# Reading turned blocks back later, attending later still, and sending some blocks through GpSimd's DMA queue

## The chip, the core and the metric

The kernel runs on one core of one Trainium2 chip. TensorE (PE) multiplies, VectorE (DVE) and ScalarE (ACT) work elementwise, GpSimd (POOL) does a little of both, and SyncE (SP) issues nearly all DMAs. The five run at once, each through its own instructions in order, and wait for each other by semaphores. The metric is the device time of one execution in microseconds; 408.61 us is the median of three runs before the change (406.73 to 408.71).

## The reference

One decoder layer, all float32, 256 tokens of width 1024. The projection gives u (512 wide) and q, k, v of 8 attention heads of width 64. u goes through a causal pooling mixer. The sequence is one block of 256, so that the attention is plain causal attention within it.

```python
z = h @ w_in[l]
pool_out = multiscale_pool(u, w_pool[l], pool_scale[l])
attn_out = moba_attention(q, k, v).reshape(B_, S_, ATTN_WIDTH)
mix = jnp.concatenate([pool_out, attn_out], axis=-1) @ w_out[l]
h = layer_norm(DEEPNORM_ALPHA * h + mix, ln1_g[l], ln1_b[l])
h = layer_norm(DEEPNORM_ALPHA * h + memory_cross_attention(h, mem, w_xq[l], w_xkv[l], w_xo[l]), ...)
h = layer_norm(DEEPNORM_ALPHA * h + swiglu(h, w_gate[l], w_up[l], w_down[l]), ln3_g[l], ln3_b[l])
```

The cross-attention has 4 heads of width 256 over 256 memory tokens. The SwiGLU is 2816 wide.

## The kernel before

Precision. A float32 product is made of three faster ones: each operand is split into a high part (a cast on ACT) and a low part (a difference on DVE), and PE multiplies high by high, high by low and low by high. `split` (L318) does this for activations, `Stream.prepare` (L87) for weights.

Weights. All of them are one `Stream` of chunks of 512 KB. A chunk is loaded by SP into one of 7 raw buffers (w20r, say), cast by ACT (w20h, L99), differenced by DVE (w20l, L100). The load of chunk i + 7 (L80) is issued when chunk i is split, since it takes its raw buffer. So the order in which the splits stand on DVE sets when SP can go on, and whatever stands behind such a load on SP waits with it. Chunks w15 to w18 belong to u, w19 to w26 to xk (the memory's keys), w27 to w34 to the output projection of the mixer, w35 to w42 to xv (the memory's values), w43 to w50 to the queries of the cross heads, w51 to w58 to their output projection, w59 and up to the SwiGLU.

Order. Nothing is scheduled: engines run the instructions in the order in which the Python code emits them. Each projection is a generator that yields after a step, and `run(gen, n)` emits n steps. For u, xk and the queries a step is 3 matmuls, for xv 6. Other work is emitted between such calls, so that the sequence of `run` calls (L548 to L589, L707 to L721, L773 to L804) is a hand-written order for all engines at once.

The hop. PE wants some matrices with the other axis on the partitions. Instead of transposing them on PE, the kernel lets DVE turn 32x32 blocks, writes them to HBM with one DMA, and reads them back with four, which put the blocks at their places: `turned` (L335) and `landed` (L346). All these DMAs are on SP's queue, among the weight loads. It is done for the mixer's attention probabilities, by pairs of heads (ps is turned, pd is the copy in HBM, pt what is read back; `probs_out`, `probs_in`, `attend`), for the two 128-token halves of norm 1's output (hs, hd, hr; `h1_out`, `h1_in`, `h1_split`), and for cross heads 0 and 1 (xs, xd, xr; `xprobs_out`, `xprobs_in`, `xprobs_split`). Cross heads 2 and 3 are transposed by PE (`xprobs_pe`, L756).

Stages. q and k; then v; then u and xk with the attention's scores, hops and products (`attend`, the po tiles) and the pooling (`pool_diff`, `mix_pool`) between their steps; the mixer's output projection; norm 1 on DVE while PE goes on with xv; the queries of the four cross heads (pxq), each with its scores (xs), softmax and hop; the products with xv (xo) between steps of the cross output projection; norm 2; SwiGLU; norm 3. The memory's activations are split in two halves (`split_mem(0)`, `split_mem(4)`, tiles mTh and mTl), of which each xk chunk pair wants both. A norm (`Norm`, L597) takes its sums out of PE's banks, and its power of -1/2 (L622) is made on POOL, whose only other work behind the start is the pooling's window sums (L508, L510).

Of the kernel before, what the change touches and what calls it, by code (L numbers as in the profile page):

```python
# [18 lines left out]
KD = D // P  # L19
# [106 lines left out]
def decoder_layer(  # L126
# [3 lines left out]
    nc = tc.nc  # L130
# [78 lines left out]
    def split_mem(k):  # L209
        split(mT[0][:, k:k + 4, :], mT[1][:, k:k + 4, :], mr[0][:, k:k + 4, :])  # L210
# [99 lines left out]
    def run(gen, n=None):  # L310

        while n is None or n > 0:
            if next(gen, gen) is gen:
                return False
            n = None if n is None else n - 1
        return True

    def split(h, l, ps):  # L318
        nc.scalar.copy(h, ps)  # L319
        nc.vector.tensor_sub(l, ps, r32(h))  # L320
# [11 lines left out]
        split(dst[0][:, k0:k0 + 4, ts], dst[1][:, k0:k0 + 4, ts], ps.rearrange("p (k t) -> p k t", k=4))  # L332


    def turned(blocks, n, name):  # L335

        st = sp.tile([P, 4, n, 32], F32, name=f"{name}s", tag="pair", bufs=3)
        for at, src in blocks:
            m = src.shape[1]
            nc.vector.transpose(st[:, :, at:at + m, :].rearrange("p j m b -> p m j b"),  # L340
                                src.rearrange("p m (j b) -> p m j b", b=32))
        via = hp.tile([P, 4, n * 32], F32, name=f"{name}d")
        nc.sync.dma_start(via, st.rearrange("p j m b -> p j (m b)"))
        return via

    def landed(via, n, name, raw=None):  # L346

        if raw is None:
            raw = sp.tile([P, 4, n, 32], F32, name=f"{name}r", tag="pair", bufs=3)
        for j in range(4):  # L350
            nc.sync.dma_start(raw[32 * j:32 * (j + 1)].rearrange("p i m b -> p i (m b)"),
                              via[:, j, :].rearrange("(i a) r -> a i r", i=4))
        return raw

# [91 lines left out]
    def scores(hq, t):  # L446
        w = (t + 1) * P
        pss = [bank(f"ps{j}").rearrange("p (h s) -> p h s", h=2) for j in range(2)]
        for h in range(2):
            for j in range(2):  # L450
                hs = slice(j * HD, (j + 1) * HD)
                hp = 2 * hq + h
                nc.tensor.matmul(pss[j][:, h, :w], qT[hs, hp, t * P:(t + 1) * P], kT[hs, hp, :w],
                                 start=True, stop=True)
        todo = []
        for j in range(2):
            pr = sp.tile([P, 2, S], F32, name="pr", bufs=PR_BUFS)[:, :, :w]
            mx = sp.tile([P, 2], F32, name="mx", bufs=6)
            for h in range(2):
                nc.vector.tensor_tensor_reduce(pr[:, h, :], pss[j][:, h, :w], tri[:, S - w:], -1.0, -NEG,  # L460
                                               op0=OP.add, op1=OP.min, accum_out=mx[:, h:h + 1])
            todo.append((pr, exps(pr, pr, mx, -1.0)))
            probs[hq, t, j] = pr
        for pr, sm in todo:
            scaled(pr, sm)
# [6 lines left out]
    def probs_out(hp):  # L472
        blocks = []
        for j in range(2):
            for t in range(T):
                pr = probs[hp // 2, t, j][:, hp % 2]
                blocks.append((3 * j + t, pr.rearrange("p (m c) -> p m c", c=P)))
        turns[hp] = turned(blocks, 6, "p")

    def probs_in(hp):  # L480
        if hp % 2 == 0:
            homes[hp // 2] = ap.tile([P, 2, KD * P], F32, tag="a8", name=f"pt{hp // 2}")
        raw = homes[hp // 2][:, hp % 2, :4 * 6 * 32].rearrange("p (i m b) -> p i m b", i=4, m=6)
        raw = landed(turns[hp], 6, "p", raw).rearrange("p i m b -> p m i b")
        pts[hp] = [(raw[:, 3 * j:3 * j + 2], raw[:, 3 * j + 2]) for j in range(2)]
# [3 lines left out]
    def attend(hp):  # L489
        po = bank("po")  # L490
        for j in range(2):
            hs = slice(j * HD, (j + 1) * HD)
            vs = slice((2 * hp + j) * HD, (2 * hp + j + 1) * HD)
            s0, s1 = pts[hp][j]
            out = po[hs, :S].rearrange("p (t i b) -> p t i b", t=T, i=4)
            nc.tensor.matmul(out, vt[:, 0, vs], s0, start=True, stop=False)  # L496
            nc.tensor.matmul(out[:, 1], vt[:, 1, vs], s1, start=False, stop=True)  # L497
        split(cT[0][:, 4 + hp, :], cT[1][:, 4 + hp, :], po[:, :S])
# [14 lines left out]
    def pool_diff(g):  # L513
        pl = upad[:, g, PADW:]
        nc.vector.scalar_tensor_tensor(pl, sums[g][:, PADW:], 1.0 / WINDOWS[g], pl, op0=OP.mult, op1=OP.subtract)

    def mix_pool(g):
        pm = bank("pm")
        nc.tensor.matmul(pm[:, :S], wpl[:, g, :], upad[:, g, PADW:], start=True, stop=True)
        nc.scalar.activation(cT[0][:, g, :], pm[:, :S], AF.Copy, bias=0.0, scale=psc[:, g:g + 1])  # L520
        nc.vector.scalar_tensor_tensor(cT[1][:, g, :], pm[:, :S], psc[:, g:g + 1],
                                       r32(cT[0][:, g, :]), op0=OP.mult, op1=OP.subtract)
# [25 lines left out]
    v, u, xk = do_v(), do_u(), do_xk()  # L548
# [3 lines left out]
    run(v, 4)  # L552
    scores(0, 1)
    run(v)
    probs_out(0)
    run(u, 6)
    scores(1, 0)
    probs_in(0)
    probs_out(1)
    run(u, 10)  # L560
    scores(1, 1)
    probs_in(1)
    split_mem(0)
    run(u, 8)
    attend(0)
    pool_diff(0)
    pool_diff(1)
    run(u, 4)
    probs_out(2)
    split_mem(4)  # L570
    run(u)
    attend(1)
    run(xk, 12)
    probs_in(2)
    probs_out(3)
    mix_pool(0)
    run(xk, 8)
    mix_pool(1)
    pool_diff(2)
    probs_in(3)  # L580
    run(xk, 8)
    attend(2)
    mix_pool(2)
    pool_diff(3)
    ws.pace = 2
    run(xk, 10)
    attend(3)
    mix_pool(3)
    run(xk)  # L589
    ws.pace = 1  # L590

# [54 lines left out]
    def project(chunks, get, held, pieces=PIECES):  # L646

        acc = {piece: accbank("acc") for piece in PIECES}  # L650
        if pieces != PIECES:
            (*_, (_, _, c), _), last = pieces, PIECES[-1]
            acc[pieces[-2]], acc[pieces[-1]] = acc[last][:, :c - last[1]], bank("acc")[:, :last[2] - c]
        head, rest = chunks[:-held], chunks[-held:]
        done = sum(ws.rows(numbers) for numbers in head)
        if head:
            yield from proj_rows(acc, head, get, PIECES, True, pieces != PIECES, True)
        ws.prepare(ws.used + AHEAD)
        ws.prepare(ws.used + W_BUFS, nc.gpsimd)
        ws.held = True  # L660
        for piece in pieces:
            yield from proj_rows(acc, rest, lambda k: get(done + k), [piece], not head or piece[1] % 512 != 0, True,
                                 piece == pieces[-1], bool(head) and pieces != PIECES)
            yield piece, acc[last] if pieces != PIECES and piece == pieces[-2] else acc[piece]
# [8 lines left out]
    load_norm("g", 1, ln1_g)()  # L673
    load_norm("b", 1, ln1_b)()
    h1 = ap.tile([P, T, D], F32, tag="a8", name="h1")
    mix = project(c_mix, lambda k: (cT[0][:, k], cT[1][:, k]), 4)
    for t in range(T):
        norm = Norm(1, xt[:, t, :], h1[:, t, :])
        for half in HALVES:
            norm.add(*half, until(mix)[1])  # L680
        norm.finish()
    run(mix)
    ws.held = False
    h1T = (a8("h1Th", F32R), a8("h1Tl", F32R))
# [7 lines left out]
        for t, c0, c1 in PIECES:  # L692
            split(xv[0][:, t, c0:c1], xv[1][:, t, c0:c1], acc[t, c0, c1])

    def h1_out(t):
        via[t] = turned([(0, h1[:, t, :].rearrange("p (k b) -> p k b", k=KD))], KD, "h")

    def h1_in(t):
        via[t] = landed(via[t], KD, "h")

    def h1_split(t):
        raw = via[t].rearrange("p i k b -> p k i b")
# [1 line left out]
            h, l = [h[:, k0:k0 + 4, t * P:(t + 1) * P].rearrange("p k (i b) -> p k i b", i=4) for h in h1T]  # L704
            split(h, l, raw[:, k0:k0 + 4])

    via = {}  # L707
    gv = do_xv()
    run(gv, 1)
    h1_out(0)  # L710
    run(gv, 3)
    h1_in(0)
    run(gv, 2)
    h1_out(1)
    run(gv, 2)
    h1_split(0)
    run(gv, 1)
    h1_in(1)
    run(gv, 3)
    h1_split(1)  # L720
    run(gv)  # L721

# [2 lines left out]
    xqT, xpr, xpt = {}, {}, {}  # L725
# [16 lines left out]
        xpr[h] = pr  # L742

    def xprobs_out(h):
        via[h] = turned([(0, xpr[h].rearrange("p s t b -> p (s t) b"))], 4, "x")

    def xprobs_in(h):
        via[h] = landed(via[h], 4, "x")

    def xprobs_split(h):  # L750
        raw = via[h].rearrange("p i m b -> p m i b")
# [21 lines left out]
    xq = [do_xq(h) for h in range(XH)]  # L773
# [4 lines left out]
    xprobs_out(0)  # L778
    run(xq[2], 5)
    xscores(1)  # L780
    run(xq[2], 3)
    xprobs_in(0)
    run(xq[2])
    xprobs_out(1)
    run(xq[3], 5)
    xprobs_split(0)
    xscores(2)
    xprobs_in(1)
    run(xq[3], 1)
    xattend(0)  # L790
    run(xq[3])

    h2 = ap.tile([P, T, D], F32, tag="a8", name="h2")
    xo = project(c_xo, lambda k: (oT[0][:, k], oT[1][:, k]), 4)
    xprobs_split(1)
    xprobs_pe(2)
    run(xo, 3)
    xscores(3)
    xattend(1)
    xattend(2)  # L800
    run(xo, 3)
    xprobs_pe(3)
    run(xo, 2)
    xattend(3)  # L804


# [149 lines left out]
```

## Time and profile before

| | |
|---|---|
| median of three runs | 408.61 us (406.73 to 408.71) |
| the profiled execution | 408.14 us, span 406.4 us |
| PE busy | 376.0 us, 93% |
| DVE, ACT, POOL busy | 254.6, 178.3, 18.0 us |
| mean granted clock of PE | 0.969 of full |
| DMA | 78.21 MB, mean 192 GB/s; 77.48 MB of it on SP's queue |

The span is from the first instruction to the last; the execution's own time is 1.7 us more. Starts and durations in a timeline are in us from the span's start. A value in brackets is how long the engine stood idle before that instruction, with what ended the wait; where the named engine had long been done, it was another, often a DMA. SPq is SP's queue of instructions: its rows give the time that the issue took, not the transfer. The grouped list of DMAs gives the median time from issue to landing. In a row of a stretch, the busy time of PE, its weight loads, DVE, ACT and POOL is followed by PE's granted clock, the share of the 16 DMA engines and the GB/s.

### The profile page before, as it was taken

How to read it: one execution, taken by the hardware profiler on the slowest of the kernel's cores; microseconds unless marked ns; L12 is line 12 of the kernel's file. 1: busy time of each engine (PE TensorE's matmuls, PEld its weight loads, DVE VectorE, ACT ScalarE, POOL GpSimd, SP SyncE). 2: the span in 40 equal slices, each digit the busy share in tenths (PEclk: the TensorE clock that was granted, in tenths of full speed). 3: DMA queues.
4: the chain of work that ended last, by engine and by line, in shares of the span. 5: the costliest groups of instructions: out<-in, count | busy, mean ns of one | idle time of the engine just before them, and what ended most of it. 6: DMA issues, size and time to landing. Idle time of an engine off the chain costs nothing.

```text
span 406.4 us, 5467 instructions
## 1 busy us (share of the span) xinstructions
PE 376.0 (93%) x2072; PEld 325.8 (80%) x2072; DVE 254.6 (63%) x376; ACT 178.3 (44%) x259; POOL 18.0 (4%) x31
## 2 busy tenths in 40 slices
PE   9999954999999719999999999999999999999992
PEld 9997953999888519999887888888888888888882
DVE  5768985665489328676488965555555464544165
ACT  4757572364342226545414654444544444334100
POOL 1000055000010000000000000000000000000000
PEclk9999996999999958999999999999999999999997
DMA  8995878767606975554210984545556655440002
GB/s 256 414 411 188 248 257 259 234 204 255 234 21 188 348 239 195 198 179 156 104 52 6 334 330 166 200 166 197 184 185 239 230 199 185 178 155 0 2 23 80
DMA packets 27225, 78.21 MB, mean 192 GB/s; under 512 B 3136, under 2 KB 8384, under 8 KB 27072
## 3 DMA queue, kind: packets, MB, share of 16 engines
q1 hardware_dynamic: 26624, 77.48, 54.9%
q10 hardware_dynamic: 576, 0.39, 0.3%
q8 instruction: 16, 0.26, 0.3%
q14 instruction: 9, 0.07, 0.1%
HBM read 73.66 MB, written 4.19 MB: 192 GB/s over the span
## 4 chain that ended last, share of the span: by engine, by line
PE 59%; DVE 5%; DMA 5%; issue 1%; ACT 0%; SPq 0%; DVEq 0%; ACTq 0%
PE pg L256 9%; PE pg L258 9%; PE pg L257 9%; PE acc L258 7%; PE acc L257 7%; PE acc L256 7%; PE pxq L274 6%; DMA w49r<-in_w_xq 2%; DMA hd<-hs 2%; PE pgt L837 1%; DMA hr<-hd 1%; DVE st L614 1%; DVE h L633 1%; PE xo L257 1%; DVE r L627 1%
## 5 line engine op out<-in xcount | busy, mean ns | idle before, releaser
L622 POOL TENSOR_TENSOR rs<-rs,mhalf 128x1 f32<-128x1 f32 x6 | 5.4, 892 | 328.2 <-DVE rs L621 328.2
L830 ACT ACTIVATE sg<-pg 128x256 f32<-128x256 f32 x22 | 8.4, 384 | 12.9 <-PE pg L258 12.8
L274 PE MATMUL pxq<-h1Th,w43h 128*128 128x256 f32 x8 | 3.4, 420 | 11.1 <-ACT h1Th L319 11.1
L496 PE MATMUL po<-pt,vt 128*64 128x256 f32 x16 | 3.1, 465 | 10.1 <-DMA pt<-pd 8.0
L611 DVE SCALAR_TENSOR_TENSOR r<-h,acc 128x256 f32<-128x256 f32 (+1 forms) x10 | 5.1, 520 | 10.9 <-PE acc L258 10.9
L831 DVE TENSOR_TENSOR sg<-sg,pg 128x256 f32<-128x256 f32 x22 | 9.3, 421 | 4.0 <-ACT sg L830 2.6
L274 PEld LDWEIGHTS pxq<-h1Th,w43h 128*128 128x128 f32 x8 | 2.6, 320 | 11.5 <-ACT h1Th L319 11.5
L320 DVE TENSOR_TENSOR h1Tl<-hr,h1Th 128x512 fp32r<-128x512 f32 x4 | 2.6, 688 | 14.0 <-ACT h1Th L319 14.0
L319 ACT CAST h1Th<-hr 128x512 fp32r<-128x512 f32 x4 | 2.3, 616 | 19.9 <-DMA hr<-hd 19.9
L429 ACT ACTIVATE pr<-pr,mx 128x128 f32<-128x128 f32 (+1 forms) x16 | 7.1, 444 | 7.3 <-DVE mx L460 7.3
L496 PEld LDWEIGHTS po<-pt,vt 128*64 128x64 f32 x16 | 1.0, 152 | 10.7 <-issue 8.2
L319 ACT CAST gTh<-pgt 128x512 fp32r<-128x512 f32 x11 | 6.0, 589 | 5.8 <-PE pgt L837 5.8
L614 DVE BATCH_NORM_STATS2 st<-r 128x6 f32<-128x512 f32 (+1 forms) x14 | 8.1, 580 | 0.5
L320 DVE TENSOR_TENSOR gTl<-pgt,gTh 128x512 fp32r<-128x512 f32 x11 | 7.1, 687 | 2.0 <-ACT gTh L319 1.5
L319 ACT CAST h2Th<-tp 128x512 fp32r<-128x512 f32 x4 | 2.3, 587 | 13.5 <-PE tp L330 13.4
L429 ACT ACTIVATE xpr<-xs,mx 128x256 f32<-128x256 f32 x8 | 3.7, 470 | 9.5 <-DVE mx L440 9.5
L627 DVE SCALAR_TENSOR_TENSOR r<-r,mv,g 128x512 f32<-128x512 f32 x11 | 7.8, 744 | 0.0
L319 ACT CAST cTh<-po 128x256 fp32r<-128x256 f32 x4 | 1.5, 372 | 12.7 <-PE po L497 12.7
L508 POOL TENSOR_TENSOR win<-upad 128x271 f32<-128x271 f32 x4 | 3.9, 968 | 53.3 <-ACT upad L536 53.3
L837 PEld LDWEIGHTS pgt<-ident,sg 128*128 128x128 f32 x44 | 5.2, 140 | 0.8
L837 PE MATMUL pgt<-ident,sg 128*128 128x128 f32 x44 | 5.8, 272 | 0.0
L633 DVE SCALAR_TENSOR_TENSOR h<-r,rs,b 128x512 f32<-128x512 f32 x8 | 5.6, 746 | 0.0
(1089 smaller groups left out, 1425.6 us busy)
## 6 DMA issues: line engine op xcount, KB each, us to landing
pd<-ps SPq DMA_DIRECT2D x4, 384.0 KB, 6.1
pt<-pd SPq DMA_DIRECT2D x16, 96.0 KB, 3.7
g<-in_ln_g SPq DMA_DIRECT2D x3, 512.0 KB, 5.1
b<-in_ln_b SPq DMA_DIRECT2D x3, 512.0 KB, 5.9
wr<-in_w_qkv SPq DMA_DIRECT2D x5, 256.0 KB, 4.2
mr<-in_mem_t SPq DMA_DIRECT2D x1, 1024.0 KB, 10.8
xt<-in_x SPq DMA_DIRECT2D x1, 1024.0 KB, 7.2
hd<-hs SPq DMA_DIRECT2D x2, 512.0 KB, 5.8
```

The lines of the kernel that those rows point to most:

```text
L256: nc.tensor.matmul(ps, wa, ya, start=start, stop=False, skip_group_check=part)
L257: nc.tensor.matmul(ps, wa, yb, start=False, stop=False, skip_group_check=part)
L258: nc.tensor.matmul(ps, wb, ya, start=False, stop=stop, skip_group_check=part)
L274: nc.tensor.matmul(pss[f], w[:, s], y, start=k == 0 and f == 0 and n == 0, stop=k == KD - 1 and n == 2, skip_group_check=True)
L319: nc.scalar.copy(h, ps)
L320: nc.vector.tensor_sub(l, ps, r32(h))
L429: nc.scalar.activation(dst[:, j, :], src[:, j, :], AF.Exp, bias=mx[:, j:j + 1], scale=sign, accum_out=sm[:, j:j + 1])
L614: nc.vector.bn_stats(self.st[:, self.n, :], self.r[:, c0:c1])
L627: nc.vector.scalar_tensor_tensor(r, r, self.mv[:, 0:1], gb["g", self.i][:, s], op0=OP.subtract, op1=OP.mult)
L633: nc.vector.scalar_tensor_tensor(self.dst[:, s], r, self.rs, gb["b", self.i][:, s], op0=OP.mult, op1=OP.add)
L831: nc.vector.tensor_mul(sg, sg, ps[:, CW:])
L837: nc.tensor.transpose(pt[:, f, t * P:(t + 1) * P], sgs[c][:, t, f * P:(f + 1) * P], ident)
```

## The change

It has three parts. First, in the mixer, `scores(1, 0)` and `probs_out(0)` change places, the reads `probs_in` come later, and the products `attend` later still: before, pairs 0 and 1 are attended among u's steps and at xk's start; now after 12 and 16 steps of xk. `split_mem(4)` comes earlier, ahead of the first pooling differences. Second, norm 1's halves are turned and written right behind each half's norm instead of among xv's steps, and these DMAs, reads too, are issued by GpSimd. Third, cross heads 0, 1 and now 2 hop, all through GpSimd's queue; head 2 is not transposed by PE any more, and the products with xv stand later: head 0's behind the last query chunk, head 1's behind four steps of the output projection, heads 2 and 3 together at its end.

```diff
-    def turned(blocks, n, name):
+    def turned(blocks, n, name, queue=nc.sync):
...
-        nc.sync.dma_start(via, st.rearrange("p j m b -> p j (m b)"))
+        queue.dma_start(via, st.rearrange("p j m b -> p j (m b)"))
...
-    def landed(via, n, name, raw=None):
+    def landed(via, n, name, raw=None, queue=nc.sync):
...
-            nc.sync.dma_start(raw[32 * j:32 * (j + 1)].rearrange("p i m b -> p i (m b)"),
+            queue.dma_start(raw[32 * j:32 * (j + 1)].rearrange("p i m b -> p i (m b)"),
...
     run(v)
+    run(u, 6)
+    scores(1, 0)
     probs_out(0)
     run(u, 6)
-    scores(1, 0)
-    probs_in(0)
     probs_out(1)
-    run(u, 10)
     scores(1, 1)
-    probs_in(1)
     split_mem(0)
     run(u, 8)
-    attend(0)
+    probs_in(0)
+    run(u, 4)
+    split_mem(4)
     pool_diff(0)
     pool_diff(1)
     run(u, 4)
+    probs_in(1)
+    run(u)
+    run(xk, 4)
     probs_out(2)
-    split_mem(4)
-    run(u)
+    run(xk, 8)
+    mix_pool(0)
+    probs_out(3)
+    attend(0)
+    run(xk, 4)
     attend(1)
-    run(xk, 12)
-    probs_in(2)
-    probs_out(3)
-    mix_pool(0)
-    run(xk, 8)
+    run(xk, 4)
     mix_pool(1)
     pool_diff(2)
+    probs_in(2)
+    run(xk, 4)
     probs_in(3)
-    run(xk, 8)
-    attend(2)
+    run(xk, 6)
     mix_pool(2)
     pool_diff(3)
     ws.pace = 2
-    run(xk, 10)
+    run(xk, 8)
+    attend(2)
+    mix_pool(3)
+    run(xk, 8)
     attend(3)
-    mix_pool(3)
...
+    via = {}
+
+    def h1_out(t):
+        via[t] = turned([(0, h1[:, t, :].rearrange("p (k b) -> p k b", k=KD))], KD, "h", nc.gpsimd)
+
+    def h1_in(t):
+        via[t] = landed(via[t], KD, "h", queue=nc.gpsimd)
+
...
         norm.finish()
+        h1_out(t)
+        if t == 1:
+            h1_in(0)
+    h1_in(1)
     run(mix)
...
-    via = {}
     gv = do_xv()
-    run(gv, 1)
-    h1_out(0)
-    run(gv, 3)
-    h1_in(0)
-    run(gv, 2)
-    h1_out(1)
-    run(gv, 2)
+    run(gv, 7)
     h1_split(0)
-    run(gv, 1)
-    h1_in(1)
-    run(gv, 3)
+    run(gv, 5)
     h1_split(1)
...
-        via[h] = turned([(0, xpr[h].rearrange("p s t b -> p (s t) b"))], 4, "x")
+        via[h] = turned([(0, xpr[h].rearrange("p s t b -> p (s t) b"))], 4, "x", nc.gpsimd)
...
-        via[h] = landed(via[h], 4, "x")
+        via[h] = landed(via[h], 4, "x", queue=nc.gpsimd)
...
     xscores(1)
-    run(xq[2], 3)
     xprobs_in(0)
     run(xq[2])
     xprobs_out(1)
     run(xq[3], 5)
-    xprobs_split(0)
     xscores(2)
     xprobs_in(1)
-    run(xq[3], 1)
-    xattend(0)
+    xprobs_split(0)
     run(xq[3])
+    xprobs_out(2)
...
+    xattend(0)
     xprobs_split(1)
-    xprobs_pe(2)
-    run(xo, 3)
     xscores(3)
+    xprobs_in(2)
+    run(xo, 4)
     xattend(1)
-    xattend(2)
-    run(xo, 3)
+    run(xo, 2)
+    xprobs_split(2)
     xprobs_pe(3)
     run(xo, 2)
+    xattend(2)
     xattend(3)
```

On SP, in the mixer, between the last chunks of xk and the first of the output projection: `-` rows stand there before, `+` rows now (pd is a pair's write, pt its four reads, xt the residual stream).

```order
 L80 DMA w25r<-in_w_xk 128x1024
-L343 DMA pd<-ps 128x768
 L80 DMA w26r<-in_w_xk 128x1024
-L351 DMA pt_634<-pd 32x4x192 x4
 L343 DMA pd<-ps 128x768
 L190 DMA xt<-in_x 128x2x1024
 L80 DMA w27r<-in_w_out 128x1024
+L343 DMA pd<-ps 128x768
 L80 DMA w28r<-in_w_out 128x1024
-L351 DMA pt_634<-pd 32x4x192 x4
 L80 DMA w29r<-in_w_out 128x1024
+L351 DMA pt_740<-pd 32x4x192 x4
```

Pair 0's reads moved from behind w26 to behind w29; pair 1's, which stood behind w28, now stand behind w30.

On POOL, from the end of the pooling to the end of the program (rs is a norm's power; hd and xd are writes, hr and xr reads):

```order
 L510 TENSOR_TENSOR win<-win,fac 128x16
-L622 TENSOR_TENSOR rs<-rs,mhalf 128x1 x6
-L952 UNCONDITIONAL_BRANCH
-L952 ISA
+L627 TENSOR_TENSOR rs<-rs,mhalf 128x1
+L343 DMA hd<-hs 128x1024
+L627 TENSOR_TENSOR rs<-rs,mhalf 128x1
+L343 DMA hd<-hs 128x1024
+L351 DMA hr<-hd 32x4x256 x8
+L343 DMA xd<-xs 128x512
+L351 DMA xr<-xd 32x4x128 x4
+L343 DMA xd<-xs 128x512
```

Where POOL had six small instructions left, it now also issues the hops of norm 1 and of three cross heads in this one order; block 1's write stands ahead of block 0's reads.

On ACT, in the cross heads, around the exponentials of head 2 and of head 3 (xst is the split of a hop's block, oTh that of a product, xq that of a query chunk):

```order
 L99 CAST w56h<-w56r 128x1024
+L429 ACTIVATE xpr,sm<-xs,mx 128x2x128 x2
+L319 CAST xst<-xr 128x512
+L99 CAST w57h<-w57r 128x1024
+L323 ACTIVATE xq_1867<-pxq 128x512
+L319 CAST oTh<-xo 128x512
 L319 CAST xst<-xr 128x512
 L429 ACTIVATE xpr,sm<-xs,mx 128x2x128 x2
+L99 CAST w58h<-w58r 128x1024
+L99 CAST w59h<-w59r 128x1024
 L319 CAST oTh<-xo 128x512
```

Head 0's block is now split behind head 2's exponentials, and head 1's ahead of head 3's.

More of the change, by code (lines that the diff above doesn't have):

```diff
@@ L693, in do_xv @@
             split(xv[0][:, t, c0:c1], xv[1][:, t, c0:c1], acc[t, c0, c1])
[L695 to L699, printed above, removed]
     def h1_split(t):
```

## The prediction

> **What bounds the kernel now.** TensorE (PE) is busy for 93% of the span, so I read first the list of what PE waited for (total us, times, longest). Three waits are all that matter in it.
>
> ```profile
> PE 376.0 (93%) x2072; PEld 325.8 (80%) x2072; DVE 254.6 (63%) x376; ACT 178.3 (44%) x259; POOL 18.0 (4%) x31
> PE pxq L274 <- ACT h1Th L319: 11.1, 1, 11.1
> PE po L496 <- DMA pt<-pd: 8.0, 1, 8.0
> PE po L496 <- ACT upad L536: 2.1, 1, 2.1
> ```
>
> Second, PE's timeline around them (start, duration, instruction; the wait in brackets):
>
> ```profile
> 54.74 0.66 PE L496 MATMUL po<-pt,vt 128*64 128x256 f32 x4 [2.08 <-ACT upad L536]
> 55.55 0.38 PE L274 MATMUL pu<-xTh,w18h 128*128 128x256 f32 x1
> 58.39 0.28 PE L274 MATMUL pu<-xTh,w18l 128*128 128x256 f32 x1
> 66.68 1.13 PE L496 MATMUL po<-pt,vt 128*64 128x256 f32 x4 [8.01 <-DMA pt<-pd]
> 68.16 0.58 PE L274 MATMUL pxk<-mTh,w19h 128*128 128x256 f32 x1
> 72.25 0.28 PE L274 MATMUL pxk<-mTh,w20h 128*128 128x256 f32 x1
> 87.47 0.28 PE L274 MATMUL pxk<-mTh,w24h 128*128 128x256 f32 x1
> 90.35 0.28 PE L274 MATMUL pxk<-mTh,w25h 128*128 128x256 f32 x1
> 139.43 0.39 PE L258 MATMUL xv<-w42h,mTl 128*128 128x512 f32 x1
> 150.88 0.58 PE L274 MATMUL pxq<-h1Th,w43h 128*128 128x256 f32 x1 [11.07 <-ACT h1Th L319]
> 156.41 0.29 PE L274 MATMUL pxq<-h1Th,w44h 128*128 128x256 f32 x1
> ```
>
> The long waits also leave PE on a slow clock. One chunk's 24 matmuls take 2.88 us at full clock (w24: 87.47 to 90.35), but w19's take 4.09 after the 8.01 us wait and w43's 5.53 after the 11.07; the second attention (66.68 to 68.16) takes 1.48 where the first took 0.81. After the wait of 2.08 nothing is slow. So the attention site holds 2.08 + 8.01 + (4.09 - 2.88) + (1.48 - 0.81) = 11.97 us and the norm 1 site 11.07 + (5.53 - 2.88) = 13.72: 25.7 us in all.
>
> Why the operands come late stands in SP's and DVE's timelines:
>
> ```profile
> 53.17 0.43 SPq L190 DMA_DIRECT2D xt<-in_x  x1
> 54.28 0.44 SPq L80 DMA_DIRECT2D w28r<-in_w_out  x1
> 55.49 2.36 SPq L351 DMA_DIRECT2D pt<-pd  x4
> 125.19 0.33 SPq L343 DMA_DIRECT2D hd<-hs  x1
> 136.86 0.33 SPq L343 DMA_DIRECT2D hd<-hs  x1
> 144.16 1.75 SPq L351 DMA_DIRECT2D hr<-hd  x4
> 121.46 1.41 DVE L633 SCALAR_TENSOR_TENSOR h<-r,rs,b 128x512 f32<-128x512 f32 x2
> 130.73 1.24 DVE L340 STREAM_TRANSPOSE hs<-h 128x1024 f32<-128x1024 f32 x1
> ```
>
> Pair 1's four reads (55.49 to 57.85) are queued behind xt (1 MB) and two weight loads, and PE gets them 8.8 us after the last was issued. Norm 1's second block was turned by 131.97, but SP, which issues in order, sends it at 136.86 and reads it back at 144.16. Third, stretches of the span (the last two columns are the share of the DMA engines and GB/s) show them idle just before that and then full:
>
> ```profile
> 114.00:124.00 10.00, 10.00 (x45) 8.27 (x45) 9.79 (x19) 5.43 (x6) 1.98 (x2) 1.00 0.01 2
> 126.00:140.00 14.00, 13.81 (x61) 11.10 (x60) 7.21 (x8) 1.85 (x3) 0.00 (x0) 1.00 1.02 304
> 136.00:138.00 2.00, 2.00 (x10) 1.66 (x9) 0.00 (x0) 0.00 (x0) 0.00 (x0) 1.00 1.15 238
> ```
>
> **The change, part by part.** All times below are on the clock of before, each site by itself.
>
> *Attention in the mixer.* No work is added; reads and products move. PE now runs through u without attending and ends it at 58.51 - 2.08 - 0.81 = 55.6, where xk starts on the first half of mem's split:
>
> ```profile
> 54.27 1.23 DVE L320 TENSOR_TENSOR mTl<-mr,mTh 128x1024 fp32r<-128x1024 f32 x1
> ```
>
> DVE has as much to do ahead of that row as before, so it ends at about 55.4; then come w21l (56.5), w22l (57.6) and the second half (58.8), 1.1 us each. xk wants the second half after one chunk, at 58.5: a wait of some 0.4. SP holds w28 until w21's raw buffer is free (56.6) and w29 until w22's (57.7). Behind these two stand pair 0's four reads, at 2.4 us for four: 58.1 to 60.5. Ahead of their data is 1.05 MB, 3.5 us from 56.6 at some 300 GB/s, then their own 0.39 MB: landed about 63. PE, after 12 steps of 0.36 us, arrives at 60.4 and waits 2.6. Pair 1's reads follow w30 (w23's buffer, free at 61.3 behind two pooled differences): issued to 64.1, landed near 66; PE comes at 65.3, waits about 1. So 4.0 us of new waits, each of the length after which the clock stayed full. Gain 11.97 - 4.0 = 8.0. Bounds: no wait (12.0), or reads as late as pair 1's were, 8.8 us after the last issue (about 0). I lie nearer the first, because xt, half of what stood ahead of pair 1's reads, is now issued some 8 us before pair 0's. Pairs 2 and 3 are read from about 70 and 72.5 and attended near 77 and 81: landed in time.
>
> *Norm 1's blocks.* Block 0 is turned right behind its own norm and written by GpSimd at about 118.4, into idle DMA engines. Both transposes (1.15 us apart) now stand ahead of DVE's next weight chunk: block 1 is ready at 122.87 + 2.3 = 125.2 instead of 131.97, and waits for no load on SP. xv's matmuls that want the banks whose sums the first transpose delays lose 0.3; w39l comes 2.3 us later, at 126.3; xv, which ends at 139.66, needs it four chunks of 2.72 us before that, at 128.8, so this is hidden. The unknown price is c, the time GpSimd spends on issuing one DMA. SP's pieces take 2.36 / 4 or 1.75 / 4 = 0.44 to 0.59. The trace holds no DMA of GpSimd; its instructions run from 0.22 to 1.49:
>
> ```profile
> 59.43 1.49 POOL L508 TENSOR_TENSOR win<-upad 128x271 f32<-128x271 f32 x1 [0.60 <-ACT upad L536]
> 63.27 1.08 POOL L510 TENSOR_TENSOR win<-win,fac 128x16 f32<-128x16 f32 x1
> 67.26 0.22 POOL L510 TENSOR_TENSOR win<-win,fac 128x16 f32<-128x16 f32 x1
> 120.30 0.99 POOL L622 TENSOR_TENSOR rs<-rs,mhalf 128x1 f32<-128x1 f32 x1 [4.74 <-DVE rs L621]
> ```
>
> I take c = 1.0, the one-element power being nearest to an instruction that is all overhead; bounds 0.44 and 1.49. From 126.3 on, block 1's write and both reads are 1.57 MB, 6.6 us at the 238 GB/s of the window in which the second write ran alone in front. Weight loads fill the same engines from 126, so I give the hop half of them: done at 126.3 + 13.2 = 139.5, then two casts on ACT and a difference on DVE, 1.8 us: 141.3. PE ends xv at 139.66 and waits 1.7, clock kept. Gain 13.72 - 1.7 - 0.3 = 11.7. Bounds: a hop not slowed by the loads (13.4), and the landings of before, us after issue:
>
> ```profile
> hd<-hs SPq DMA_DIRECT2D x2, 512.0 KB, 5.8
> hr<-hd SPq DMA_DIRECT2D x8, 128.0 KB, 6.3
> ```
>
> With these, block 1 lands at 126.3 + 5.8 + 4c + 6.3 = 142.4, is split at 144.2, and PE waits 4.5: gain 8.9, or 6.3 if the clock falls. [...]
>
> *Cross heads.* Three heads' blocks (15 DMAs) go through GpSimd. Head 2's PE transposes (0.44 us) and a wait of 0.36 go away; one cover is lost:
>
> ```profile
> 177.93 0.39 PE L257 MATMUL xo<-xst,xv 128*128 128x256 f32 x1 [0.36 <-DVE xst L320]
> 182.95 0.60 PE L760 MATMUL xpt<-ident,xpr 128*128 128x128 f32 x4
> 192.01 0.59 ACT L319 CAST oTh<-xo 128x512 fp32r<-128x512 f32 x1 [0.66 <-PE xo L258]
> 192.63 0.69 DVE L320 TENSOR_TENSOR oTl<-xo,oTh 128x512 fp32r<-128x512 f32 x1 [0.30 <-ACT oTh L319]
> 168.66 0.33 SPq L343 DMA_DIRECT2D xd<-xs  x1
> xd<-xs SPq DMA_DIRECT2D x2, 256.0 KB, 2.1
> xr<-xd SPq DMA_DIRECT2D x8, 64.0 KB, 3.2
> ```
>
> After head 1's product the output projection wants that product's split at once. In these rows the split runs from 192.01 to 193.32, some 0.2 us behind the product; PE can fill 0.46 of it with two matmuls that need only the cast: 1.1 shows. Net cost 1.1 - 0.8 = 0.3. Whether the DMAs stay covered hangs on c. Head 0's product, moved behind the last query chunk, is wanted at 182.95 - 2.06 = 180.9; head 1's two products of 1.44 and four steps of 1.37 later, at 189.2; head 2's at 197.7; each less 1.3 for the split. From 168.66, head 0 takes 5c + 5.3, head 1 10c + 7.4, head 2 15c + 9.5 (one or more landings of 2.1, one of 3.2): hidden up to c of about 1.1 to 1.2. At 1.0 that holds, narrowly; above it each 0.1 costs 1.5 us.
>
> **Sum.** 8.0 + 11.7 - 0.3 = 19.4. The profiled execution took 408.14 us (span 406.4), 0.1% below the median of 408.61: 408.14 - 19.4 = 388.7, so **389**.
>
> **Rivals.**
> 1. *The attention reads stay late.* For: SP still sends them behind w28, w29 and w30. Against: xt is gone from ahead of them. Waits of 5.5 and 1.5 and the slow clock's 1.9 instead of 4.0: **394**. Chance 0.12.
> 2. *DVE's work slows GpSimd's DMAs.* For: the 16-element multiply took 1.08 beside DVE's subtractions and 0.22 with DVE idle. If issuing pays those 0.86 where DVE is busy (63% of the span), c is 1.0 + 0.54, say 1.6: block 1's last read is issued at 125.3 + 9c = 139.7, landed at 141.7, split at 143.5, 3.8 late; head 2 is 15c + 9.5 - 27.7 = 5.8 late: 408.14 - 8.0 - 9.6 + 6.1 = **397**. Against: the multiply reads SBUF as DVE does, an issue may not. Chance 0.16. [...]
> 3. *Slower than before: GpSimd's issuing becomes the bound.* At c = 2.5, h1 is split at 125.3 + 22.5 + 3.8 = 151.6, as late as now, and head 2 is 19.3 late: 408.14 - 8.0 + 19.6 = **420**. It decides from c of about 2.0, where h1's wait costs 10.1 and head 2's 11.8. For: 25 DMAs stand in one in-order queue. Against: no GpSimd row exceeds 1.49. Chance 0.09.
>
> **How the numbers follow.** The forecast has 0.63, its own range is 384 to 394. All 25.7 gone and nothing new would be 383; rival 2 with the slow clock as well is 400, and c of 1.8 is 402. So 384 to 402, which leaves out rival 3 and little else. About 0.5% (2 us) is what a measurement here can tell from no change; part of rival 3 lies there. Faster 0.89, same 0.03, slower 0.08.
>
> **What would show it.** Right: PE's wait list holds attention waits under 3 us and one for h1Th under 3; the chunks w19 and w43 take about 2.9 us; hd is issued about 1 us after its block is turned, the first into idle DMA engines. Wrong: GpSimd's DMAs over 1.2 us apart, PE waiting for xst, a chunk at 4 us behind a wait, or attention's reads landing 5 us or more after their last issue.

## The result, and the profile after

The changed kernel takes 395.26 us, the median of four runs (393.81 to 397.28): 0.969 of the kernel before, with a 95% interval of 0.964 to 0.975. Six more runs of it, later, gave 395.86 (393.71 to 398.09; 0.970, 0.966 to 0.974). The kernel before, run beside it, had a median of 408.16 (four runs). The forecast was 389, its range 384 to 402: faster, as forecast, but the change removed 12 to 13 us and not 19. The profiled execution took 395.94 us (span 394.2).

What PE waited for in the changed kernel (total us, times, longest):

```profile
PE po L496 <- DMA pt<-pd: 6.0, 3, 3.1
PE pxq L274 <- ACT h1Th L319: 2.1, 1, 2.1
PE pxk L274 <- DVE mTl L320: 0.7, 1, 0.7
PE acc L256 <- ACT oTh L319: 0.7, 1, 0.7
```

The three waits of before (11.1, 8.0 and 2.1) are gone. There are three new ones for the attention's reads where the prediction had two, and one for h1T. PE's timeline has them in their places, and the first matmuls of five chunks that bound the stages:

```profile
41.67 0.28 PE L274 MATMUL pu<-xTh,w15h 128*128 128x256 f32 x1
64.35 0.87 PE L496 MATMUL po<-pt,vt 128*64 128x256 f32 x4 [3.12 <-DMA pt<-pd]
65.58 0.58 PE L274 MATMUL pxk<-mTh,w20h 128*128 128x256 f32 x1
68.08 0.28 PE L274 MATMUL pxk<-mTh,w20l 128*128 128x256 f32 x1
69.55 0.66 PE L496 MATMUL po<-pt,vt 128*64 128x256 f32 x4 [1.19 <-DMA pt<-pd]
81.07 0.66 PE L496 MATMUL po<-pt,vt 128*64 128x256 f32 x4 [1.69 <-DMA pt<-pd]
92.75 0.40 PE L256 MATMUL acc<-w27h,cTh 128*128 128x512 f32 x1
114.53 0.39 PE L256 MATMUL xv<-w35h,mTh 128*128 128x512 f32 x1
139.14 0.38 PE L274 MATMUL pxq<-h1Th,w43h 128*128 128x256 f32 x1 [2.11 <-ACT h1Th L319]
139.87 0.58 PE L274 MATMUL pxq<-h1Tl,w43h 128*128 128x256 f32 x1 [0.35 <-DVE h1Tl L320]
144.17 0.28 PE L274 MATMUL pxq<-h1Th,w44h 128*128 128x256 f32 x1
200.28 0.48 PE L256 MATMUL pg<-w59h,h2Th 128*128 128x512 f32 x1
```

The same bounds in the kernel before (w44's row, 156.41, stands in the prediction):

```profile
41.78 0.28 PE L274 MATMUL pu<-xTh,w15h 128*128 128x256 f32 x1
96.11 0.40 PE L256 MATMUL acc<-w27h,cTh 128*128 128x512 f32 x1
117.89 0.39 PE L256 MATMUL xv<-w35h,mTh 128*128 128x512 f32 x1
212.27 0.48 PE L256 MATMUL pg<-w59h,h2Th 128*128 128x512 f32 x1
```

So the mixer with attention (w15 to w27) went from 54.33 to 51.08 us, the stage of norm 1 (w35 to w44) from 38.52 to 29.64, and the cross heads (w44 to w59) from 55.86 to 56.11. Against a forecast of 8.0, 11.7 and -0.3 that is 3.25, 8.88 and -0.25. The missing 7.5 us of the trace are in the first two stages: 4.7 and 2.8.

### The profile page after: what moved, and what is told of

The parts are those of the page before. It is cut to its first block, busy times and chain, and to the rows that moved or that the text cites. A ratio compares the mean times of both kernels' runs of the same rounds, so it can differ in the third digit from the quotient of the medians.

```text
span 394.2 us, 5486 instructions
## 1 busy us (share of the span) xinstructions
PE 375.6 (95%) x2068; PEld 325.0 (82%) x2068; DVE 257.2 (65%) x377; ACT 177.8 (45%) x259; POOL 34.1 (9%) x56
## 4 chain that ended last, share of the span: by engine, by line
PE 80%; DMA 7%; DVE 7%; issue 2%; ACT 2%; SPq 1%; POOL 1%; DVEq 0%; ACTq 0%; POOLq 0%
PE pg L258 10%; PE pg L256 10%; PE pg L257 10%; PE acc L256 8%; PE acc L258 8%; PE acc L257 8%; PE pxq L274 6%; PE pqk L392 6%; DMA hr<-hd 3%; PE pxk L274 2%; DMA pt<-pd 2%; PE pgt L840 1%; PE busy L363 1%; PE pv L256 1%; PE pv L257 1%
## 5 line engine op out<-in xcount | busy, mean ns | idle before, releaser
L351 POOL DMA_DIRECT2D xr<-xd x12 | 6.5, 550 | 7.6 <-DVE sm L434 2.8
L508 POOL TENSOR_TENSOR win<-win 128x269 f32<-128x269 f32 (+2 forms) x6 | 6.6, 1100 | 0.5
L320 DVE TENSOR_TENSOR oTl<-xo,oTh 128x512 fp32r<-128x512 f32 x4 | 2.8, 692 | 4.9 <-ACT oTh L319 4.8
L434 DVE RECIPROCAL sm<-sm 128x2 f32<-128x2 f32 x12 | 2.0, 166 | 5.8 <-ACT xpr L429 4.3
```

The costliest lines, as they stand in the source:

```text
L508: nc.gpsimd.tensor_add(nxt[:, 2 * n - 1:], cur[:, 2 * n - 1:], cur[:, n - 1:PADW + S - n])
```

## The experiments

All kernels below compute the whole layer. The time is the median with its range, the ratio is to the kernel before, and the stages are read from one trace of each, as above.

| kernel | us | ratio, 95% interval | w15-w27 | w35-w44 | w44-w59 |
|---|---|---|---|---|---|
| before | 407.2 to 408.2 by batch | | 54.33 | 38.52 | 55.86 |
| the mixer's order alone | 403.97 (402.50-407.39) | 0.993, 0.991-0.995 | 50.78 | 38.17 | 55.57 |
| norm 1's hop alone | 398.91 (398.12-400.56) | 0.980, 0.978-0.983 | 54.20 | 31.72 | 55.57 |
| cross heads alone | 408.50 (405.45-411.44) | 1.004, 1.001-1.007 | 53.41 | 38.02 | 56.32 |
| after | 395.26 (393.81-397.28) | 0.969, 0.964-0.975 | 51.08 | 29.64 | 56.11 |
| after, again | 395.86 (393.71-398.09) | 0.970, 0.966-0.974 | 52.04 | 30.07 | 56.05 |
| norm 1's hop on SP | 394.59 (393.40-395.86) | 0.970, 0.968-0.973 | 52.77 | 27.01 | 56.53 |
| hop on GpSimd, loads held | 400.03 (399.37-402.72) | 0.982, 0.978-0.987 | 51.13 | 34.04 | 56.13 |
| waits filled | 395.27 (394.28-396.33) | 0.969, 0.966-0.973 | 50.71 | 28.65 | 56.76 |
| attention's reads early | 392.66 (392.04-393.47) | 0.963, 0.960-0.966 | 48.56 | 29.73 | 56.05 |
| both early | 390.21 (389.73-390.86) | 0.957, 0.954-0.960 | 48.62 | 25.19 | 58.00 |
| both early, two more moves | 390.90 (390.33-395.18) | 0.961, 0.956-0.966 | 49.30 | 25.20 | 57.09 |
| the same, old cross heads | 390.37 (389.21-391.45) | 0.957, 0.954-0.961 | 49.79 | 25.20 | 56.49 |
| the same, attention into the mix | 384.84 (384.22-385.28) | 0.943, 0.940-0.946 | 43.16 | 25.22 | 56.49 |

### The three parts, each alone

Each kernel is the one before with one part of the diff. Expected of the mixer, of norm 1 and of the cross heads:

> The kernel before with the new order in the mixer alone. From the two traces the stage from the first u chunk to the first chunk of the mixer's output projection (w15 to w27) became 54.33 - 51.08 = 3.25 us shorter, with waits of 0.73, 3.12, 1.19 and 1.69 us and half-clock matmuls that cost 1.6 us in place of the 11.97 removed. If the parts add up, 408.2 - 3.3 = 404.9 us (403 to 407, since the half clock may or may not come). Rival: the three attention waits come from GpSimd's hops or anything else outside the mixer; then they are absent and the stage is 8 us shorter, 400.

> The kernel before with norm 1's blocks turned early and moved by GpSimd, alone. From the traces of before and after (w35 to w44: 38.52 against 29.64 us) 408.2 - 8.9 = 399.3 us (397.5 to 401). PE waits 2 to 3 us for h1Th. Rival: the parts do not add up, since weight loads stand elsewhere in time; then the wait for h1Th differs by more than 2 us from 2.1.

> The kernel before with the three cross heads' hops through GpSimd and their products later, alone. From the traces (w44 to w59: 55.86 against 56.11 us) 408.2 + 0.2 = 408.4 us: no difference that can be measured (407.5 to 409.5). Rival: the hops cost or save something that the other two parts hide; then it is 1 us or more away from 408.2.

Measured: 3 us, 8 us and no gain or a small loss, in that order. The mixer's waits are its own, since waits of 3.87 and 1.05 us for the attention's reads stand there without GpSimd's hops. The three ratios multiply to 0.977, while the whole is 0.969, so the parts seem to do more together than apart, by some 3 us; the intervals of the four ratios allow almost as much error. Norm 1's stage holds two of them in the traces: alone it had a wait of 3.50 us for h1Th and the half clock over nearly the whole chunk of w43, and its reads took 10.7 us in the median, not 9.1. Why these were slower there is open. The cross heads' stage is 56.05 to 56.32 us in the kernels that have the new order and are otherwise undisturbed, and 55.57 to 55.86 in those with the old: a loss of about half a microsecond, where 0.3 was forecast.

### Norm 1: the queue, or what else it carries

In the kernel after, GpSimd issued both blocks' reads by 128.15, yet the second was cast only at 138.47. SP had meanwhile begun to send weights. Rows of GpSimd's, SP's and ACT's timeline, and the grouped DMAs (median us from issue to landing last):

```profile
122.94 2.23 POOL L351 DMA_DIRECT2D hr<-hd  x4
125.98 2.17 POOL L351 DMA_DIRECT2D hr<-hd  x4 [0.82 <-DMA hd<-hs]
123.18 0.33 SPq L80 DMA_DIRECT2D w46r<-in_w_xq  x1
134.06 1.14 ACT L319 CAST h1Th<-hr 128x512 fp32r<-128x512 f32 x2 [9.54 <-DMA hr<-hd]
138.47 1.14 ACT L319 CAST h1Th<-hr 128x512 fp32r<-128x512 f32 x2 [0.51 <-DMA hr<-hd]
hr<-hd POOLq DMA_DIRECT2D x8, 128.0 KB, 9.1
```

A stretch of that time (the last column is GB/s):

```profile
128.00:132.00 4.00, 4.00 (x19) 3.31 (x18) 1.97 (x2) 0.00 (x0) 0.15 (x1) 1.00 1.00 247
```

The same program with these ten DMAs on SP, where they stand ahead of w46:

```diff
-        via[t] = turned([...], KD, "h", nc.gpsimd)
+        via[t] = turned([...], KD, "h")
-        via[t] = landed(via[t], KD, "h", queue=nc.gpsimd)
+        via[t] = landed(via[t], KD, "h")
```

> The kernel after, with norm 1's two writes and eight reads issued by SP at the same place of the program instead of by GpSimd; there they stand ahead of the load of w46 and all later ones. Theory (the hop's 1.6 MB shared the DMA engines with w46 to w52, which SP issues from 123.2 us on): with these loads behind it in one queue, block 1 lands near 133 instead of 138.5, PE's wait of 2.08 + 0.35 us for h1T and the half clock behind it (1.8) go, and the time is 395.3 - 4.2 = 391 us. Rival 1 (a hop's landing is a fixed latency, whichever the queue and the company): as after, 395. Rival 2 (the queue of its own is what made the hop early): SP, which waits for the block's write before it reads, holds the weight loads up by 5 us, queries wait for w46 and the time is 398 or more.

In the grouped DMAs of this kernel the reads land in 3.6 us:

```profile
hr<-hd SPq DMA_DIRECT2D x8, 128.0 KB, 3.6
```

The stage became 27.01 us: no half clock there, and 2.6 us shorter, of the 4.2 expected. PE still waited 0.30 and 0.96 us for h1T, because the second block's cast stood on ACT behind w46 and w47, of which one now waited for its late load and the other for PE (ACT's timeline of this kernel):

```profile
134.33 1.05 ACT L99 CAST w46h<-w46r 128x1024 fp32r<-128x1024 f32 x1 [3.47 <-DMA w46r<-in_w_xq]
137.49 1.05 ACT L99 CAST w47h<-w47r 128x1024 fp32r<-128x1024 f32 x1 [2.11 <-PE xv L258]
138.44 1.13 ACT L319 CAST h1Th<-hr 128x512 fp32r<-128x512 f32 x2
```

The time, 394.59, cannot be told from the kernel after, and 391 was expected. In the one trace the mixer was 1.7 us longer than in the first one of after, with the same code; the stages of the other runs are not known. That run changed the queue and the company of the reads at once. To part them, the reads went back to GpSimd and the weights were held instead:

```diff
     h1_in(1)
+    gate = hp.tile([P, 4], F32, name="gate")
+    nc.sync.dma_start(gate, via[1][:, 0, 0, 0:4])
     run(mix)
```

> The kernel after, with norm 1's hop on GpSimd as there, and one small write of block 1's first four columns to HBM put on SP ahead of the load of w46: SP sends it, and with it w46 and all later weights, only when block 1 has landed. It takes the weight loads away from beside GpSimd's reads and changes nothing else about them. Theory (the 9.1 us that a read took in the kernel after are the weight loads' share of the DMA engines): the reads land in 3.5 to 5 us, as SP's own did with nothing beside them (3.6), block 1 by about 133. Rival (reads that GpSimd issues are slow by themselves): 9 us again, as after. The time is not what this run is for: w46 comes later still, 393 to 399.

The same row of this kernel's grouped DMAs:

```profile
hr<-hd POOLq DMA_DIRECT2D x8, 128.0 KB, 4.3
```

4.3 us: the issuer adds 0.7, the weight loads beside it 4.8. (The loads start at 131 here, too late for ACT, hence the time.) So a queue of its own freed the reads from SP's order, not from SP's traffic: 9.1 us beside the loads, 4.3 without them.

### The half clock behind a short wait

The prediction took waits of under 3 us as harmless to PE's clock, since one of 2.08 had been so. In the kernel after, the clock halved behind 3.12 us and behind 2.11. In the traces of before and after the clock's changes lie whole steps of 3.41 us apart (before: it fell at 63.88 and at 142.39, 23 steps; after: at 64.66 and at 139.75, 22 steps). Cut along this grid, stretches show what stood ahead of the falls (length, then busy PE, ..., the granted clock third from the end). Before, after, after again, and norm 1 alone:

```profile
53.64:57.05 3.41, 2.31 (x20) 2.10 (x21) 3.09 (x5) 3.41 (x6) 2.10 (x2) 1.00 0.83 232
57.05:60.47 3.42, 1.62 (x14) 1.42 (x12) 2.59 (x6) 2.30 (x3) 2.66 (x5) 1.00 0.99 374
60.47:63.88 3.41, 0.00 (x0) 0.00 (x0) 3.41 (x6) 0.00 (x0) 3.17 (x4) 1.00 1.07 282
```

```profile
61.25:64.66 3.41, 0.31 (x4) 0.31 (x6) 3.41 (x3) 0.75 (x2) 3.17 (x4) 1.00 0.58 139
64.66:68.07 3.41, 3.41 (x19) 2.96 (x16) 3.41 (x7) 0.37 (x1) 3.17 (x5) 0.50 0.98 269
78.31:81.73 3.42, 1.73 (x17) 1.45 (x16) 1.48 (x2) 0.48 (x1) 0.00 (x0) 1.00 0.94 259
136.34:139.75 3.41, 1.07 (x5) 0.41 (x3) 2.84 (x4) 2.32 (x4) 0.00 (x0) 1.00 1.01 339
139.75:143.17 3.42, 3.30 (x15) 3.30 (x16) 3.25 (x5) 3.42 (x6) 0.00 (x0) 0.50 1.03 410
```

```profile
59.02:62.43 3.41, 1.23 (x9) 0.82 (x7) 2.64 (x3) 2.00 (x3) 3.17 (x5) 1.00 0.91 230
62.43:65.85 3.42, 1.33 (x8) 0.89 (x8) 3.42 (x6) 0.00 (x0) 3.18 (x5) 0.50 0.92 258
```

```profile
56.57:59.98 3.41, 1.42 (x12) 1.22 (x11) 2.58 (x6) 2.09 (x3) 2.69 (x4) 1.00 0.97 376
59.98:63.39 3.41, 0.00 (x0) 0.00 (x0) 3.41 (x6) 0.00 (x0) 3.17 (x4) 0.50 1.07 290
```

A stretch at full clock in which PE was busy for 1.42 us or less was followed by the half clock, one with 1.62 or more was not: so in these rows, and in every other stretch of the traces of before and after between 50 and 160 us. The 2.08 us of before (52.66 to 54.74) lay across a grid line at 53.64, the 2.11 of after (137.03 to 139.14) within one stretch. The same program's clock fell at 64.66 in one execution and at 62.43 in another, where it stayed down for longer: there the next stretch held 1.33 us of busy PE, against 3.41.

Is that where 3.4 of the missing 7.5 us went? Idle matmuls in the waits should keep the clock up and delay nothing:

```diff
     probs_out(3)
+    keep_busy(12)
     attend(0)
...
     run(gv)
+    keep_busy(8)
```

> The kernel after, with 12 idle matmuls (128x128, nothing reads them) ahead of the first attention product and 8 ahead of the first query chunk: they lie in time in which PE waited 3.12 and 2.08 us, so they shift nothing. Theory (the half clock behind these waits comes from the waits themselves, which leave too little work in one of the clock's windows): the granted clock stays at 1.00 at both places, w20's and w43's matmuls keep 0.12 us each, and the time is 395.3 - 1.6 - 1.8 = 392 us, with the waits themselves as long as before less the filling. Rival (the matmuls there are slow for another reason, the traffic of weights or the late split): w43's chunk stays at 4.7 us or more and the time at 395.

> The kernel after, once more, beside the runs above: 393.8 to 397.3 as measured, 395.3. If the half clock comes and goes with where a wait falls in the clock's windows, its trace can show other places of half clock than the first trace (64.6 to 68.1 and 139.8 to 143.2 us) with the same program.

The two places in the filled kernel (the granted clock is again the third from the end):

```profile
61.00:71.00 10.00, 6.87 (x59) 6.04 (x59) 9.63 (x16) 1.91 (x6) 7.81 (x8) 1.00 0.91 249
136.00:146.00 10.00, 8.88 (x72) 8.46 (x71) 9.27 (x11) 8.26 (x12) 0.00 (x0) 1.00 1.02 382
```

The clock stays at 1.00 (busy PE: 6.87 and 8.88 us, against 5.69 and 7.54 in the same stretches of after, at 0.83), so the cause of the slow matmuls is as the theory says. The 3.4 us do not come: 395.27, as after. What PE gains it spends at the next operand. The filled kernel's timeline of PE:

```profile
65.01 0.66 PE L496 MATMUL po<-pt,vt 128*64 128x256 f32 x4 [1.45 <-DMA pt<-pd]
69.19 0.66 PE L496 MATMUL po<-pt,vt 128*64 128x256 f32 x4 [1.68 <-DMA pt<-pd]
148.01 0.39 PE L258 MATMUL xs<-xkTh,xq 128*128 128x256 f32 x1 [0.47 <-DVE xq L324]
```

Pair 1's product starts 27.88 us behind w15's first matmul in both traces (69.55 - 41.67; 69.19, where w15 starts at 41.31), and 28.63 in the second trace of after: its reads land about then, and a PE at full clock only waits longer. Pair 0's product cannot be compared so: it starts 22.68 and 23.84 us behind w15 in the two traces of after, and 23.70 here. In norm 1's stage 1.0 us comes, and 0.65 of it goes again in the cross heads, where DVE is late with the first query. The spread of the six runs is smaller with the filling: 2.1 us between the fastest and the slowest instead of 4.4.

### Reads ahead of loads

Where the attention's waits come from stands in SP's and DVE's timelines of the kernel after:

```profile
58.46 1.80 SPq L351 DMA_DIRECT2D pt<-pd  x4
63.61 1.85 SPq L351 DMA_DIRECT2D pt<-pd  x4
73.56 0.33 SPq L80 DMA_DIRECT2D w34r<-in_w_out  x1
73.98 2.69 SPq L351 DMA_DIRECT2D pt<-pd  x4
56.45 1.56 DVE L100 TENSOR_TENSOR w22l<-w22r,w22h 128x1024 fp32r<-128x1024 f32 x1
67.15 1.65 DVE L100 TENSOR_TENSOR w26l<-w26r,w26h 128x1024 fp32r<-128x1024 f32 x1
72.31 1.23 DVE L100 TENSOR_TENSOR w27l<-w27r,w27h 128x1024 fp32r<-128x1024 f32 x1 [0.25 <-ACT w27h L99]
```

Pairs 0 and 1 are used 4.1 us after the last issue of their reads (60.26 to 64.35, 65.46 to 69.55). Pair 2's reads stand behind the load of w34, and that behind w27's difference, which DVE ends at 73.5. So the reads were moved ahead of the loads, and the products behind:

```diff
     split_mem(0)
-    run(u, 8)
     probs_in(0)
+    probs_in(1)
     run(u, 4)
     split_mem(4)
+    run(u, 8)
...
-    probs_in(1)
...
     probs_out(3)
+    run(xk, 4)
     attend(0)
     run(xk, 4)
     attend(1)
-    run(xk, 4)
     mix_pool(1)
...
     run(xk, 8)
-    attend(2)
     mix_pool(3)
     run(xk, 8)
+    attend(2)
+    run(xk, 8)
     attend(3)
     run(xk)
```

> The kernel after, with the reads of pairs 0 and 1 on SP ahead of the loads of w28 and w29 instead of behind w29 and w30, the second half of mem's split one weight chunk earlier, and the four attention products 4, 4, 8 and 8 xk steps later. Theory (the attention's waits are the distance between SP's turn and PE's, nothing else): pair 0 lands near 60, pair 1 near 62, PE arrives at 61 and 63.5, and the waits of 0.73, 3.12, 1.19, 1.69 and the half clock's 1.6 go: 395.3 - 8.3 = 387 us. Rival (the transfers take as long as DMA traffic lets them, and reads put ahead only push weight loads into the same stretch): waits of 2 us or more stay at pt or move to xk's weights, 391 to 395.

The three waits for attention's reads and the one for mem's second half went, but only 2.5 us of the stage, not 8.3. The list of PE's waits has a new one:

```profile
PE pm L519 <- DVE upad L515: 3.9, 1, 3.9
```

It is the third pooled product, which wants a difference that DVE makes at 72.32, in the middle of work without a pause. The attention's waits had hidden it. With norm 1's reads on SP as well, and the second block's split ahead of w46 and w47 on ACT and DVE (`h1_split(1)` right behind `h1_split(0)`):

> attn_early, and norm 1's DMAs on SP ahead of w46 (as in norm1_sp), and its second block's split on ACT and DVE ahead of the weight chunks w46 and w47. In norm1_sp the block had landed some 4 us before its cast, which stood behind those two chunks, and PE still waited 1.0 + 0.3 us. Theory: no wait for h1T and no half clock: 395.3 - 8.3 - 4.2 = 383 us. Rival (the loads of w46 and on, 5 us later, are wanted in time by the queries): PE waits for w46 to w48, 385 to 388.

The time is 390.21 us, not the 383 expected. No wait for h1T is left, and norm 1's stage is 25.19 us, 4.5 shorter than after; 1.9 of it go again in the cross heads:

```profile
143.41 0.39 PE L258 MATMUL xs<-xkTh,xq 128*128 128x256 f32 x1 [1.52 <-DVE xq L324]
```

The next kernel goes for both new waits (the fourth product moves by 16 steps, not 10 as the expectation has it):

```diff
-    mix_pool(2)
     pool_diff(3)
     ws.pace = 2
     run(xk, 8)
-    mix_pool(3)
+    mix_pool(2)
     run(xk, 8)
     attend(2)
     run(xk, 8)
+    mix_pool(3)
     attend(3)
...
+    ws.held = True
     run(xq[0])
+    ws.held = False
```

> both_early, with the third pooled product 8 xk steps later and the fourth 10 (in both_early PE waited 3.9 us for the third one's difference on DVE, with the half clock behind it), and with w50 and w51 prepared behind the first query's split instead of ahead of it (PE waited 1.52 us for that split). Theory (nothing else is late behind these): 390.2 - 3.9 - 1.5 - 1.5 = 383 to 384 us. Rival (DVE, which has no idle time from 53 to 77 us, is what bounds the mixer now, so the wait moves to the next operand): 387 to 390.

> best, with the cross heads as in the kernel before (two hops through SP, heads 2 and 3 transposed by PE, the old places of the products). Theory (the third part of the change costs what it removes; alone it measured +1.5 us, 0.2 to 2.7): 0 to 1.5 us faster than best. Rival (with the stages ahead shorter, SP's queue is fuller and the two hops on it come late): slower than best by 1 us or more, PE waiting for xst.

Neither kernel is faster than the last one, where 383 to 384 us was expected. The wait for the query is down to 0.37 us, but the third product's wait shrank only to 1.03, and 3.43 us (3.99 with the old cross heads) for pair 2's reads came in its place: the rival, in a new place. The old cross heads make no difference that these runs can tell. The last kernel is the one with the old cross heads, with the two late products where nothing waits for them:

```diff
-    run(xk, 8)
-    attend(2)
-    run(xk, 8)
+    run(xk, 16)
     mix_pool(3)
-    attend(3)
     run(xk)
+    attend(2)
...
+    run(mix, 4)
+    attend(3)
```

> best_oldx, with the third attention product behind the last xk step and the fourth behind four steps of the mixer's output projection, which wants neither before its second half. In best_oldx PE waited 3.99 us for pair 2's reads, and the half clock followed. Theory (these products can stand where their reads have landed, and nothing else there is late): w15 to w27 goes from 49.8 to 45 or 46 us, and the time to 386 us. Rival (DVE sets the end of the mixer): PE waits for w23 to w31's differences instead, 389 to 391.

384.84 us, 0.943 of the kernel before and 10.4 us faster than the change. The mixer's stage is 43.16 us, 6.6 shorter than in the kernel with the old cross heads; 1.2 of that came back in the output projection, where the last product now stands (w27 to w35: 22.97 us instead of 21.79). The stretch from its first xk matmul to the output projection:

```profile
54.70:84.30 29.60, 28.17 (x227) 26.32 (x225) 26.67 (x37) 17.99 (x25) 12.52 (x14) 1.00 0.95 284
```

The clock is never below 1.00 there, and PE has 1.4 us of waits left in the mixer. DVE, busy for 26.7 of 29.6 us, is close behind.

## Why the prediction was right or wrong

**The sum removed** (25.7 us) was right: no old wait and no old slow chunk is left. What came in their place was forecast at 4.0 + 2.0 and was 8.7 + 4.8 by the stages.

**mem's second half**: 0.4 forecast, 0.73. DVE took 1.56 us for w22's difference beside the window sums, not 1.1.

**Pairs 0 and 1**: SP's issuing of their reads was forecast from 58.1 to 64.1 and went from 58.46 to 65.46. The term that was too small is the landing, 2.5 and 1.9 us after the last issue, from bytes and rate; in this trace it was 4.1 both times. The waits were 3.12 and 1.19 instead of 2.6 and 1.0, which is close only because PE was late as well: luck. The landing also varies. In the five other traces in which these reads stand at the same place, pair 0's product starts 4.7 to 6.5 us behind the last issue, in three of them over the 5 us that the prediction named as a sign of being wrong, and the longest wait was 5.55 us.

**"Pairs 2 and 3 ... landed in time"** failed for pair 2: 1.69 us. The step missed is a queue position: its reads were given from about 70 and went at 73.98, behind w34's load, which hangs on DVE.

**"Each of the length after which the clock stayed full"** failed. The clock stayed full behind 2.08 us and fell behind 2.11: what went with it in the traces was not the length but how much work a stretch of the grid still held (1.42 us or less where it fell, 1.62 or more where it did not). In the trace the slow matmuls cost 1.6 us behind 64.35 (1.23 - 0.81 for the product, and 2.62 - 1.44 for twelve matmuls, from 65.58 to 68.20, where a thirteenth would have started) and 1.8 behind 139.14 (w43's chunk 5.03 - 2.88 - 0.35). But the filled kernel shows that without them the time is the same within what can be told: the slow clock stood mostly beside other lateness, and its 3.4 us would have been too much to add to the sum.

**c, GpSimd's price for one DMA**, was taken at 1.0, from the one-element power. It is 0.55 (2.23 and 2.17 for four), at the low end of the bounds, with DVE busy for all of both stretches at weight chunks' differences. So rivals 2 and 3 fall, and the cross heads' hops were hidden: no wait for xst stands in PE's list.

**"I give the hop half of them"** gave it too much. Block 1's write and both reads, the 1.57 MB of the forecast, took 16.1 us (122.35 to 138.4) and not 13.2. That is 98 GB/s of the 245 that all DMAs moved in this time, two fifths; the reads alone, 1.05 MB from 122.94 on, moved at 68, about a quarter. Counted from w35's first matmul, block 1 came 2.3 us later than forecast. That the wait, 2.11 + 0.35, still stands near the 1.7 forecast is luck: the splits cost PE 1.0 us behind the last cast's start and not 1.8, and PE ended xv 0.7 late itself. Held apart, the reads need 3.6 or 4.3 us.

**The bank and the cross heads** were about right: the chunk of w35 grew by 0.55 (forecast 0.3), the split of oT shows 0.67 us (1.1), the stage lost 0.25 to 0.5 (0.3).

**The rivals.** Rival 1, attention's reads late behind w28 to w30 (chance 0.12), is closer to what the mixer shows than the forecast: its waits and slow clock come to 8.9 us, and 8.7 stand there. Moved ahead of w28, the reads of pairs 0 and 1 were never waited for again. The prediction's lower bound for norm 1, from the landings of before, would have made 408.14 - 8.0 - 8.9 + 0.3 = 391.5 of the sum, or 394.1 with the 6.3 of a fallen clock: closer to the measured 395 than the forecast is.

## What to carry to other kernels

The waits in this profile were an upper bound: behind each removed one stood the operand that was next in lateness, and of 25.7 us here 12 came, until the work itself was moved to where its operands had landed. A transfer that must land soon belongs ahead of the bulk loads in their queue where these have time, as here (3.6 us for norm 1's reads); in a queue of their own beside the loads they took 9.1. Work that is wanted late (the last attention products) is best placed behind the wait's end rather than made to wait less: that took 6.6 us off the mixer's stage here, of which 1.2 came back.

## What the runs showed that was not expected

- The clock followed a grid of 3.41 us (the changes in before and in after lie whole steps apart), with its own phase in each execution (the first falls behind 50 us stand at 63.88 in before, 64.66 in after, 62.43 in after again and 59.98 in norm 1 alone): PE busy for 1.42 us or less of such a stretch brought the half clock for the next one, 1.62 or more did not. In the half clock, stretches with 0.00 to 1.60 us of busy PE kept it (before, 142.39 to 152.63), and those with 3.30 to 3.42 ended it (before at 70.71 and 156.04, after at 68.07 and 143.17). No long gap was needed: 2.11 us was the longest of a stretch that brought the half clock.
- GpSimd issues a DMA of 128 KB or 64 KB in 0.55 us, and what SP takes lies around it (1.80 to 2.83 us for four). In the trace of after, four took 2.23 and 2.17 us with DVE busy throughout, and 2.17 in the cross heads, where DVE was busy for 1.86 to 2.11 of them; no issue of four stands beside an idle DVE in that trace.
- Two streams did not share by halves here: norm 1's reads of 128 KB each got about a quarter of the rate beside loads of 512 KB (68 GB/s, where all DMAs moved 255 from 122.94 to 138.40). Why was not tried.
- DVE was slower beside GpSimd's window sums: differences of weight chunks take 1.22 us alone. The five from w22 (1.56) to w26 (1.65), beside GpSimd's window sums, took 7.97 us together in the changed kernel, 1.9 more than alone, in the stretch in which DVE turned out to be next in line. Either side can pay: w21's difference (55.22, 1.22 us) was not slowed beside a window sum, which took 1.31 us then and 0.64 or 0.63 later for the same shape.
